# Splitting the weights into their two parts by instructions of 1024 columns instead of 512

## Chip, cores and metric

The kernel runs on one core of a Trainium2 chip. The metric is the device time of one execution in microseconds (us), lower is better; a comparison goes by the median of several runs on one chip.

## The reference

`reference()` runs two transformer blocks, batch 1, 256 tokens of width 2048, all in fp32:

```python
# first_block, two layers, a latent stream x and a context stream ctx
hx = _rmsnorm(x, norm_g[l]) * (1.0 + scale) + shift
q, k, v, g_att, u_pool, g_pool, a_conv, b_conv, g_conv = jnp.split(hx @ w_in[l], SPLITS, axis=-1)
y = _mix(...)   # attention, pooling (w_pool) and convolution, gated, joined, then @ w_out
x = x + gate * y
...
# second_block, one layer
proj = h @ w_in[l]            # q, k, v, u, gates
merged = (jax.nn.sigmoid(gate_a) * (y_attn @ w_attn_br[l])
          + jax.nn.sigmoid(gate_s) * (y_ssm @ w_ssm_br[l]))
x = x + g1[:, None] * (merged @ w_out[l])
up = causal_dwconv(h2 @ w_up[l], conv_w[l], conv_b[l])
val, gt = jnp.split(up, 2, axis=-1)
x = x + g2[:, None] * ((jax.nn.silu(gt) * val) @ w_down[l])
```

The modulation vectors (`shift`, `scale`, `gate`) come from small products of a conditioning vector with `w_mod`. What costs time are the big matrix products with `w_in`, `w_out`, `w_up` and `w_down`.

## The kernel before

Every large product is computed to nearly fp32 accuracy with the faster fp32r matmul: a weight `w` is split into a rounded part `hi` and the rest `lo = w - hi`, the tokens likewise into `xh` and `xl`, and three products are added, `xh hi + xh lo + xl hi`. All weights are streamed. A **chunk** is 4 k-tiles of 128 rows by 512 columns (1 MB); `plan()` (L500) lists 370 of them in the order in which they are used. SyncE's queue loads a chunk into a tile `wr` (three buffers); then `_split_job` (L352) makes the tiles `wh` and `wl` (two buffers each). It goes over the four k-tiles: a copy of 512 columns on ScalarE (`act`, L168) writes `wh`, a subtraction on VectorE (`sub`, which calls `tt`, L172) reads `wr` and `wh` and writes `wl`. `chunk_b` (tokens stationary) and `chunk_a` (weights stationary) then issue the chunk's matmuls (`mm`, L153) on TensorE into PSUM banks named `mm`; with 256 tokens such a chunk is 24 matmuls of 512 columns or 32 of 512 and 256.

Beside the chunks run generators: attention heads (`attn_unit`, small PSUM banks named `sd`), the pooling branch (`pool_group`), the convolution, the S5 scan, the modulation vectors (`mod_section`: products of 1024 columns on VectorE into a tile `mv`, L192), the transpositions (`tr`, L159). All of them put instructions on the same in-order queues of TensorE, VectorE, ScalarE and GpSimd; small loads go through GpSimd's queue (`dma`, L148).

The order is fixed while the program is written, by a rough clock per engine. Each helper adds an estimate (`_adv`, L128): a ScalarE instruction 0.2 us plus columns/1150, a VectorE instruction 0.2 us plus columns/960. After each step of a chunk `pump()` (L246) lets those generators go on whose due time has come, but only while the clocks of VectorE and ScalarE are at most 2 us ahead of TensorE's. `ensure()` (L262) lets them go on until a needed value exists. `_split_later` puts the split of the next chunk into the order some 5 us ahead of its use. So the estimate that a split adds to two clocks decides beside which chunk, and in which sequence, the rest is issued:

```python
            ok = t["dve"] <= t["pe"] + slack and t["act"] <= t["pe"] + slack
...
        yield max(self.ready[k] - 1.0, self.t["pe"] + self.SPLIT)
```

The output projection `out_proj` (L1981) takes the gated outputs of the branches as its tokens. It starts with the k-tiles 8 to 11, those of the pooling branch, whose four groups run one after the other; a group ends with the matmul by its block of `w_pool`, which GpSimd's queue loads into a tile `m` (L1808), and a ScalarE copy. At the start of a layer (`pre`, `inputs`) the normed tokens are made two k-tiles at a time, by a product (L172), a ScalarE copy (L168) and an L192 step of VectorE each, just ahead of the matmuls that use them; there a chunk's matmuls go k-tile by k-tile, all four column blocks of one before the next, and elsewhere column block by column block.

Of the kernel before, what the change touches and what calls it, by code (L numbers as in the profile page):

```python
# [43 lines left out]
class Core:  # L44
    """Emission helpers: engine wrappers that keep a rough clock per engine,
    the weight stream, and generators that fill the engines beside the GEMMs."""
# [24 lines left out]
    # ---- storage  # L71
# [7 lines left out]
    def N(self, n, kind):  # L79
        """A slot of 512 columns, or half of one shared with the next tile of its kind."""  # L80
        if n == 512:
            return self.S()[:, :]
        t = self.halves.pop(kind, None)
        if t is not None:
            return t[:, 256:512]
        t = self.halves[kind] = self.S()
        return t[:, 0:256]
# [39 lines left out]
    # ---- clocks  # L127
# [10 lines left out]
    def dma_at(self, kbytes, at=0.0):  # L138
        """Rough arrival of a load of so many KB issued now."""
# [3 lines left out]
    def dma(self, out, in_, eng=None):  # L143
        """A transfer beside the weight stream; returns its rough arrival."""
# [6 lines left out]
    # ---- engines  # L151
# [59 lines left out]
    def pow_half(self, out, a):  # L211
        """out = a ** -0.5 on a few columns."""
        n = _cols(a)
# [18 lines left out]
    # ---- generators  # L232
    def side(self, gen, prio, free=False):
        """free: the generator leaves ScalarE and VectorE alone."""
# [27 lines left out]
    def ensure(self, flag):  # L262
        """Run the generators, as their steps come due, until one raises the flag."""
        n = 0
# [48 lines left out]
    # ---- weight stream  # L313
# [14 lines left out]
    RAW = 3  # L328
# [23 lines left out]
    def _split_job(self, i):  # L352
# [5 lines left out]
        for k in range(self.KC):  # L358
            h = slice(k, k + 1)
# [6 lines left out]
    def fetch(self, key):  # L366
        """The two parts of the chunk of key. Loads run up to RAW chunks ahead, and
        splits one."""
        i = self.index[key]
# [13 lines left out]
    # ---- GEMM pieces over one chunk of k-tiles and 512 columns  # L383
    def chunk_b(self, key, ps, kts, lhs, first, last, evac, pre=None):
        """Tokens stationary, weights moving: one bank [128 tokens, 512] per token tile."""
# [21 lines left out]
    def chunk_a(self, key, ps, kts, xs, first, last, evac, wide, pre=None):  # L407
        """Weights stationary: four banks of 128 columns each. xs(kt) gives (H, L) of
        512 tokens when wide, else the tile [H | L] of 256 tokens."""
# [28 lines left out]
    def total(self, ps, out=None):  # L438
        """Sum of the two halves a narrow type-A bank holds; frees the bank. Without
        out the sum stays in the first half of the tile returned."""  # L440
# [8 lines left out]
    # ---- accurate functions on small tiles  # L449
    def exp_acc(self, out, x, w):  # L450
        """out = exp(x); w(): scratch tiles of x's shape, wi(): int32 scratch."""
# [20 lines left out]
    def sincos(self, s, c, x, w):  # L472
        """s = sin(x), c = cos(x) with the argument reduced to one period."""
# [14 lines left out]
class Net(Core):  # L488
# [10 lines left out]
    # ------------------------------------------------------------ plan of weights  # L499
# [58 lines left out]
    # ------------------------------------------------------------ small vectors as columns  # L558
# [74 lines left out]
    # ------------------------------------------------------------ modulation vectors  # L633
# [7 lines left out]
    def mod_section(self, key, w, bias, vec):  # L641
        """Row vector vec @ w + bias: products and the sum over k-tiles on the vector
        engine, the sum over partitions on the tensor engine. The row is left in DRAM."""
# [42 lines left out]
    def bias_rows(self, bias):  # L686
        """A row in four blocks, block j on partitions 32 j .. 32 j + 31."""
# [5 lines left out]
    def rows_out(self, rows, ps, bt):  # L693
        """Row 32 j + i of the bank, the bias added, is block j of rows[i]."""
# [6 lines left out]
    def mod_section_pe(self, keys, w, bias):  # L701
        """Rows l1[:, :, i] @ w + bias on the tensor engine, four column blocks side by
        side in the four column groups of the array."""
# [35 lines left out]
    def mod_columns(self, keys):  # L739
        """Rows in DRAM -> columns [128, 16 per key]."""  # L740
# [17 lines left out]
    def fold_scale(self, k, g):  # L758
        """scale column <- g * (1 + scale)."""
# [50 lines left out]
    # ------------------------------------------------------------ start  # L810
# [202 lines left out]
    def row_columns(self, acc, d):  # L1013
# [3 lines left out]
        row = self.S()  # L1017
# [1554 lines left out]
```

## Time and profile before

| | us |
|---|---|
| median of 3 runs | 2985.97 |
| lowest, highest run | 2984.51, 2991.15 |
| profiled execution, from its first to its last instruction | 2987.5 |
| TensorE busy in it | 2935.2 (98%) |
| VectorE busy in it | 2085.4 (70%) |
| ScalarE busy in it | 1418.9 (47%) |
| GpSimd busy in it | 460.6 (15%) |

The page lists no time of its own for the profiled execution beside the span. A row of the timeline reads: start, length, engine, line, operation, tiles out<-in, shape, number in the group, and in brackets the idle time of the engine ahead of it with what ended it. Matmuls are pipelined, so their lengths overlap; what one costs is the distance from start to start.

### The profile page before, as it was taken

The page shows a single profiled execution, that of the slowest core. Times are in us where ns is not written, and L with a number is a line of the kernel's source. Part 1 is how long each engine was busy: PE and PEld are TensorE (multiplying, and loading weights), DVE is VectorE, ACT ScalarE, POOL GpSimd, SP SyncE. Part 2 cuts the span into 40 slices and gives each one's busy share as a digit, 9 for nine tenths or more (in the row PEclk, how much of TensorE's full clock was granted, in tenths as well). Part 3 has the DMA queues.
Part 4 walks back from the last instruction along what each step waited for, and adds up shares of the span by engine and source line. Part 5 has one row for each costly group of instructions (what it writes and reads, how often), then busy time and mean ns, then how long its engine had stood idle before and what let it go on. Part 6 is the DMA issues. An engine that isn't in the chain of part 4 may idle for free.

```text
span 2987.5 us, 40758 instructions
## 1 busy us (share of the span) xinstructions
PE 2935.2 (98%) x14636; PEld 2312.9 (77%) x14636; DVE 2085.4 (70%) x3839; ACT 1418.9 (47%) x3183; POOL 460.6 (15%) x915
## 2 busy tenths in 40 slices
PE   7999999999999999999998999999999999999999
PEld 4666667777777788788776888888778888888887
DVE  4447786635776589757786888878978777777444
ACT  4333223375452443456667554444446556555343
POOL 2000000342421000334223533200000000000000
PEclk9999999999999999999998999999999999999999
DMA  9768882426677553447686877788895555556664
GB/s 378 272 225 308 304 298 74 134 99 206 220 255 254 183 196 113 144 174 238 208 292 228 288 267 270 271 289 305 294 323 194 184 194 186 187 194 226 196 198 141
DMA packets 294534, 673.20 MB, mean 225 GB/s; under 512 B 22618, under 2 KB 23334, under 8 KB 294076
## 3 DMA queue, kind: packets, MB, share of 16 engines
q1 hardware_dynamic: 266240, 604.03, 59.6%
q0 software_dynamic: 23696, 59.53, 6.0%
q10 hardware_dynamic: 4396, 7.03, 0.6%
q8 instruction: 115, 1.88, 0.3%
q14 instruction: 87, 0.71, 0.1%
HBM read 643.65 MB, written 26.85 MB: 224 GB/s over the span
## 4 chain that ended last, share of the span: by engine, by line
PE 49%; issue 1%; DVE 1%; POOL 1%; DMA 0%; ACT 0%; POOLq 0%
PE mm L153 47%; PE sd L153 2%; PE sd L159 1%; DMA m<-in_w_pool_dram 0%; DVE s L172 0%; DVE wl L172 0%; DVE s L192 0%; POOL s L1387 0%; POOL s5w L148 0%; POOL s L148 0%; POOL rstd L214 0%; POOL s L222 0%; ACT s L168 0%; POOL c L229 0%; DVE mv L192 0%
## 5 line engine op out<-in xcount | busy, mean ns | idle before, releaser
L153 PE MATMUL mm<-wh,s 128*128 128x512 f32 x4160 | 1361.5, 401 | 2.4 <-ACT s L168 2.1
L172 DVE TENSOR_TENSOR wl<-wr,wh 128x512 fp32r<-128x512 f32 x1480 | 924.3, 686 | 502.7 <-ACT wh L168 497.4
L168 ACT ACTIVATE wh<-wr 128x512 fp32r<-128x512 f32 x1480 | 810.8, 621 | 809.7 <-PE mm L153 615.8
L153 PE MATMUL mm<-s,wh 128*128 128x512 f32 x2992 | 1034.8, 400 | 9.0 <-DVE s L192 6.2
L153 PEld LDWEIGHTS mm<-wh,s 128*128 128x128 f32 x4160 | 783.1, 188 | 214.0 <-issue 21.5
L153 PE MATMUL mm<-wl,s 128*128 128x512 f32 x2080 | 822.7, 396 | 0.0
L153 PE MATMUL mm<-s,wl 128*128 128x256 f32 (+1 forms) x2528 | 765.4, 303 | 0.0
L153 PEld LDWEIGHTS mm<-s,wh 128*128 128x128 f32 x2992 | 558.8, 190 | 189.3 <-issue 54.3
L153 PEld LDWEIGHTS mm<-s,wl 128*128 128x128 f32 x2528 | 477.7, 189 | 20.1
L153 PEld LDWEIGHTS mm<-wl,s 128*128 128x128 f32 x2080 | 392.0, 188 | 87.4 <-issue 1.0
L192 DVE SCALAR_TENSOR_TENSOR mv<-mv,vec,mv 128x1024 f32<-128x1024 f32 x210 | 268.9, 1280 | 6.2 <-DMA mv<-in_w_mod_dram 3.8
L192 DVE SCALAR_TENSOR_TENSOR s<-s,CS,s 128x254 f32<-128x254 f32 (+20 forms) x424 | 230.9, 551 | 10.9
L168 ACT ACTIVATE s<-sd 128x512 f32<-128x512 f32 (+8 forms) x298 | 114.0, 389 | 222.4 <-PE sd L159 117.6
L168 ACT ACTIVATE s<-mm 128x256 f32<-128x256 f32 (+1 forms) x220 | 101.5, 464 | 215.5 <-PE mm L153 209.8
L153 PE MATMUL sd<-s,s 128*128 128x128 f32 (+6 forms) x1248 | 184.1, 399 | 8.7 <-issue 4.9
L168 ACT ACTIVATE s<-s 128x256 f32<-128x256 f32 (+5 forms) x340 | 141.5, 442 | 86.0 <-DVE s L172 39.2
L172 DVE TENSOR_TENSOR s<-s,s 128x256 f32<-128x256 f32 (+4 forms) x304 | 148.0, 516 | 39.1 <-ACT s L168 24.8
L153 PEld LDWEIGHTS sd<-s,s 128*128 128x128 f32 (+2 forms) x1248 | 112.0, 167 | 51.7 <-issue 31.7
L172 DVE TENSOR_TENSOR s<-mm,s 128x256 f32<-128x256 f32 (+1 forms) x240 | 108.5, 481 | 50.8 <-ACT s L168 25.1
L159 PE MATMUL sd<-ident,s 128*128 128x128 f32 (+1 forms) x600 | 92.9, 276 | 16.3 <-DMA s<-in_norm_g_dram 8.6
L159 PEld LDWEIGHTS sd<-ident,s 128*128 128x128 f32 (+1 forms) x600 | 73.9, 141 | 42.1 <-issue 20.6
L218 POOL TENSOR_TENSOR c<-c,mone 128x2 f32<-128x2 f32 x56 | 49.1, 877 | 343.1 <-ACT s L168 342.8
(209 smaller groups left out, 1526.6 us busy)
## 6 DMA issues: line engine op xcount, KB each, us to landing
wr<-in_w_in_dram SPq DMA_DIRECT2D x168, 1024.0 KB, 7.0
mv<-in_w_mod_dram SPq DMA_DIRECT2D x320, 512.0 KB, 5.2
wr<-in_w_up_dram SPq DMA_DIRECT2D x88, 1024.0 KB, 5.1
wr<-in_w_out_dram SPq DMA_DIRECT2D x48, 1024.0 KB, 7.6
wr<-in_w_down_dram SPq DMA_DIRECT2D x44, 1024.0 KB, 5.2
s<-in_w_mod_dram SPq DMA_DIRECT2D x128, 256.0 KB, 5.2
s<-s5w POOLq DMA_DIRECT2D x48, 256.0 KB, 6.3
mv<-in_w_in_dram SPq DMA_DIRECT2D x16, 512.0 KB, 6.7
```

The lines of the kernel that those rows point to most:

```text
L153: self.nc.tensor.matmul(out, lhsT, rhs, start=start, stop=stop)
L159: self.nc.tensor.transpose(out, in_, self.ident[0:n, 0:n])
L168: self.nc.scalar.activation(out, in_, func, scale=scale, **kw)
L172: self.nc.vector.tensor_tensor(out, a, b, op=op)
L192: self.nc.vector.scalar_tensor_tensor(out, a, s, b, op0=op0, op1=op1)
L218: self.nc.gpsimd.tensor_tensor(out, a, b, op=op)
```

## The change

The loop of `_split_job` takes two k-tiles at a time, so that each of its instructions has 1024 columns, and there are two copies and two subtractions per chunk instead of four and four:

```diff
@@ _split_job
         t["act"] = max(t["act"], self.ready[i])
-        for k in range(self.KC):
-            h = slice(k, k + 1)
+        for k in range(0, self.KC, 2):
+            h = slice(k, k + 2)
             self.act(hi[:, h, :], raw[:, h, :])
             t["dve"] = max(t["dve"], t["act"])
             self.sub(lo[:, h, :], raw[:, h, :], hi.bitcast(F32)[:, h, :])
```

By the estimates in `act` and `tt` a split now adds 2 x (0.2 + 1024/1150) = 2.18 us to ScalarE's clock, where it added 2.58, and 2 x (0.2 + 1024/960) = 2.53 to VectorE's, where it added 2.93. So the order moves too: the same other instructions stand elsewhere, on all queues. Three places follow; the number behind a name counts tiles and differs between the two programs for the same thing.

The first place is TensorE at the end of layer 1, between the last chunk of its first half and the output projection (`mm<-wh,s` is the projection's first matmul; `m` the block of `w_pool`, or an attention output to be transposed). Before:

```order
L153 MATMUL mm_13173<-s_9192,wl_13250 128x256
L153 MATMUL sd_13413<-s_11482,s_13314 128x128
...
L159 MATMUL sd_13439<-ident,m_13293 128x128
L159 MATMUL sd_13459<-ident,m_13437 128x128
L159 MATMUL sd_13296<-ident,m_13433 128x128
L153 MATMUL sd_13468<-s_13319,m_13430 128x256
L153 MATMUL mm_13477<-wh_13342,s_13403 128x512
```

Now, first the pooling matmul (some five chunks earlier, after chunk 118 where it stood after chunk 122), then the passage to the projection:

```order
L153 MATMUL mm_12452<-s_8900,wl_12598 128x256
L153 MATMUL sd_12735<-s_12582,m_12671 128x256
L153 MATMUL mm_12749<-s_8710,wh_12683 128x512
...
L153 MATMUL sd_12962<-s_11111,s_12918 128x128
L159 MATMUL sd_12741<-ident,m_12907 128x128
L153 MATMUL mm_12777<-s_8897,wh_12876 128x512
...
L153 MATMUL mm_12786<-s_8900,wl_12877 128x256
L153 MATMUL mm_13029<-wh_12935,s_13015 128x512
```

The last pooling matmul and the last transposition of attention stood directly ahead of the projection; now other matmuls stand between. On GpSimd's queue the load of the `w_pool` block stood behind the projection's loads:

```order
L148 DMA s_13320<-in_const_inv_dram 128x256
L222 MEMSET s_13322 128x16 x2
L148 DMA s_13395<-row_gate_x 128x512
L148 DMA s_13397<-x_0_7501 128x512
L148 DMA s_13399<-x_1_7502 128x512
L148 DMA s_13401<-in_final_g_dram 128x512
L148 DMA m_13430<-in_w_pool_dram 128x128
```

Now:

```order
L148 DMA s_12583<-in_const_inv_dram 128x256
L222 MEMSET s_12585 128x16 x2
L229 TENSOR_SCALAR c_12619<-c_12619 128x1
L214 TENSOR_TENSOR c_12620<-c_12619,mhalf 128x1
L218 TENSOR_TENSOR c_12620<-c_12620,c_12239 128x1
L148 DMA m_12671<-in_w_pool_dram 128x128
```

The load is issued ahead of the projection's.

The second place is VectorE in layer 1, at the splits of chunks 76 to 78, ahead of the sums of finished banks (`s<-mm,s`). Before:

```order
L192 SCALAR_TENSOR_TENSOR mv_8583<-mv_9253,vec_145,mv_8583 128x1024
L172 TENSOR_TENSOR wl_9389<-wr_9272,wh_9388 128x512 x4
L192 SCALAR_TENSOR_TENSOR mv_8583<-mv_9323,vec_145,mv_8583 128x1024
L172 TENSOR_TENSOR wl_9436<-wr_9331,wh_9435 128x512 x4
L192 SCALAR_TENSOR_TENSOR mv_8583<-mv_9336,vec_145,mv_8583 128x1024
L192 SCALAR_TENSOR_TENSOR mv_8583<-mv_9374,vec_145,mv_8583 128x1024
L172 TENSOR_TENSOR s_9451<-mm_9274,s_9451 128x256
```

Now:

```order
L192 SCALAR_TENSOR_TENSOR mv_8316<-mv_8955,vec_145,mv_8316 128x1024
L192 SCALAR_TENSOR_TENSOR mv_8316<-mv_8971,vec_145,mv_8316 128x1024
L172 TENSOR_TENSOR wl_9088<-wr_8979,wh_9087 128x1024 x2
L192 SCALAR_TENSOR_TENSOR mv_8316<-mv_9032,vec_145,mv_8316 128x1024
L172 TENSOR_TENSOR wl_9131<-wr_9034,wh_9130 128x1024 x2
L192 SCALAR_TENSOR_TENSOR mv_8316<-mv_9058,vec_145,mv_8316 128x1024
L172 TENSOR_TENSOR s_9142<-mm_8981,s_9142 128x256
```

One modulation product of 1024 columns instead of two stands between the split and the sums.

The third place is VectorE later in the same layer, at the splits of chunks 113 and 114, where an attention head's softmax (`s<-s,c,s`, then the row maxima `c<-sd` of the next head) meets the sums of finished banks. Before:

```order
L172 TENSOR_TENSOR wl_12586<-wr_12397,wh_12585 128x512 x4
L192 SCALAR_TENSOR_TENSOR s_12538<-s_12539,c_12566,s_12538 128x512
L200 TENSOR_REDUCE c_12622<-sd_12561 128x1
L200 TENSOR_REDUCE c_12622<-sd_12562 128x1
L172 TENSOR_TENSOR wl_12640<-wr_12454,wh_12639 128x512 x4
L172 TENSOR_TENSOR s_12656<-mm_12399,s_12656 128x256
```

Now:

```order
L172 TENSOR_TENSOR wl_12185<-wr_11996,wh_12184 128x1024 x2
L196 COPY m_12223<-s_12066 128x128
L192 SCALAR_TENSOR_TENSOR mv_11204<-mv_12070,vec_145,mv_11204 128x1024
L192 SCALAR_TENSOR_TENSOR s_12052<-s_11966,s_12052 128x256
L172 TENSOR_TENSOR wl_12262<-wr_12100,wh_12261 128x1024 x2
L192 SCALAR_TENSOR_TENSOR s_12212<-s_12213,c_12240,s_12212 128x512
L172 TENSOR_TENSOR s_12274<-mm_12003,s_12274 128x256
L172 TENSOR_TENSOR s_12287<-mm_12020,s_12287 128x256
L200 TENSOR_REDUCE c_12303<-sd_12292 128x1
```

The softmax step and the maxima stood ahead of the second split; now the softmax step stands behind it and the maxima behind the sums.

## Rows read from the trace of the kernel before

**Rows 1.** The page: busy time, share of the span and instructions of each engine.

```profile
PE 2935.2 (98%) x14636; PEld 2312.9 (77%) x14636; DVE 2085.4 (70%) x3839; ACT 1418.9 (47%) x3183; POOL 460.6 (15%) x915
```

**Rows 2.** Windows: each engine's busy time, then TensorE's clock, DMA share, GB/s.

```profile
1079.60:1083.00 3.40, 3.40 (x9) 2.72 (x9) 2.52 (x6) 2.48 (x6) 0.00 (x0) 0.50 0.76 272
1420.90:1427.80 6.90, 6.64 (x29) 3.79 (x30) 4.36 (x8) 1.20 (x4) 4.94 (x11) 0.51 0.47 91
1492.60:1496.00 3.40, 3.40 (x8) 2.76 (x9) 2.88 (x7) 0.98 (x3) 0.00 (x0) 0.50 0.29 57
2400.00:2450.00 50.00, 50.00 (x288) 43.80 (x287) 35.83 (x71) 30.43 (x65) 0.00 (x0) 1.00 0.58 190
```

**Rows 3.** Groups by line and form: count, busy us, mean ns, idle before, releasers.

```profile
L172 DVE TENSOR_TENSOR wl<-wr,wh 128x512 fp32r<-128x512 f32 x1480 | 924.3, 686 | 502.7 <-ACT wh L168 497.4 <-PE sd L153 3.3 <-PE mm L153 0.4
L168 ACT ACTIVATE wh<-wr 128x512 fp32r<-128x512 f32 x1480 | 810.8, 621 | 809.7 <-PE mm L153 615.8 <-issue 177.3 <-DMA wr<-in_w_out_dram 11.2
L172 DVE TENSOR_TENSOR s<-s,s 128x512 f32<-128x512 f32 x72 | 49.5, 691 | 3.5 <-ACT s L168 1.5
L168 ACT ACTIVATE s<-s 128x256 f32<-128x256 f32 x108 | 43.8, 429 | 27.7 <-DVE s L192 13.2 <-DVE s L172 7.6 <-DVE s L188 6.8
L172 DVE TENSOR_TENSOR s<-s,s 128x256 f32<-128x256 f32 x108 | 43.8, 420 | 12.3 <-DMA s<-in_const_inv_dram 11.3
L168 ACT ACTIVATE s<-s 128x512 f32<-128x512 f32 x56 | 34.8, 625 | 35.2 <-DVE s L172 31.6 <-DVE s L188 3.1
```

**Rows 4.** Timeline of ScalarE, VectorE and TensorE at one split, chunk 73.

```profile
1044.94 2.18 ACT L168 ACTIVATE wh<-wr 128x512 fp32r<-128x512 f32 x4
1045.59 2.50 DVE L172 TENSOR_TENSOR wl<-wr,wh 128x512 fp32r<-128x512 f32 x4
1046.89 0.39 PE L153 MATMUL mm<-s,wh 128*128 128x512 f32 x1
1047.12 0.28 PE L153 MATMUL mm<-s,wl 128*128 128x256 f32 x1
```

**Rows 5.** Timeline of VectorE and TensorE at the split of chunk 74.

```profile
1051.26 2.49 DVE L172 TENSOR_TENSOR wl<-wr,wh 128x512 fp32r<-128x512 f32 x4
1052.96 0.28 PE L153 MATMUL mm<-s,wl 128*128 128x256 f32 x1
```

**Rows 6.** Timeline of TensorE at the end of layer 1.

```profile
1490.64 0.44 PE L159 MATMUL sd<-ident,m 128*128 128x128 f32 x2 [2.60 <-ACT m L168]
1492.59 1.18 PE L153 MATMUL sd<-s,m 128*128 128x256 f32 x2 [1.51 <-DMA m<-in_w_pool_dram]
```

**Rows 7.** Chain that ended last, same place: start, length, what.

```profile
1483.50 8.95 DMA m<-in_w_pool_dram
```

**Rows 8.** Timeline of VectorE and TensorE at the sums behind chunk 78.

```profile
1072.84 2.60 DVE L192 SCALAR_TENSOR_TENSOR mv<-mv,vec,mv 128x1024 f32<-128x1024 f32 x2
1079.02 0.50 PE L153 MATMUL mm<-wh,s 128*128 128x512 f32 x1 [2.12 <-ACT s L168]
```

**Rows 9.** Timeline of TensorE at 1439 us: a short idle time.

```profile
1439.25 0.47 PE L153 MATMUL mm<-s,wh 128*128 128x512 f32 x1 [0.38 <-DVE s L172]
```

**Rows 10.** Timeline of VectorE and TensorE behind the splits of chunks 113 and 114.

```profile
1417.08 1.28 DVE L200 TENSOR_REDUCE c<-sd 128x1 f32<-128x512 f32 x2
1418.28 2.49 DVE L172 TENSOR_TENSOR wl<-wr,wh 128x512 fp32r<-128x512 f32 x4
1421.16 2.40 PE L153 MATMUL sd<-s,s 64*128 64x512 f32 x4 [2.19 <-DVE s L172]
```

**Rows 11.** Timeline of VectorE and TensorE where block 2 hands over to its FFN.

```profile
2233.84 2.49 DVE L172 TENSOR_TENSOR wl<-wr,wh 128x512 fp32r<-128x512 f32 x4
2237.40 1.72 PE L153 MATMUL sd<-ident,rstd 128*128 128x128 f32 x4 [2.44 <-POOL rstd L214]
```

**Rows 12.** Timeline of TensorE behind a small burst that breaks the stream of matmuls.

```profile
2106.74 0.48 PE L153 MATMUL mm<-wh,s 128*128 128x512 f32 x1
2107.06 0.39 PE L153 MATMUL mm<-wl,s 128*128 128x512 f32 x1
```

## The prediction

> **What bounds the kernel now.** I read the page first. TensorE is busy 98% of the span, VectorE 70%, ScalarE 47% [rows 1]: 2987.5 - 2935.2 = 52 us without TensorE work is all that any change on the other engines can remove, plus what a lowered clock costs. Then the windows: in the FFN TensorE is busy 50.00 of 50 us at the full clock while VectorE has work for 35.83 and ScalarE for 30.43 [rows 2]. So where most of the time passes, the split is hidden. In the groups by line VectorE's split stands idle 502.7 us, nearly all of it for `wh`, and ScalarE's 809.7 us, most of it for a buffer that TensorE gives back [rows 3]: both wait for others, and TensorE's list of waits shows none on `wl`. What a change of the split can touch is then the handful of places where TensorE stood still. There the loss is double: behind a stall the granted clock fell to 0.50, the lower of its two levels, for 3.4 to 6.9 us [rows 2], and half of such a stretch is lost too.
>
> **The instructions themselves.** Going from 256 to 512 columns, a ScalarE copy grows from 429 to 625 ns and a VectorE operation from 420 to 691 [rows 3]. With the same slope the next 512 columns cost 392 and 542 ns: a copy of 1024 about 621 + 392 = 1013 ns, a subtraction 686 + 542 = 1228. From start to start four copies take (2.18 - 0.62)/3 = 0.52 us each and four subtractions (2.50 - 0.69)/3 = 0.60 [rows 4]; at 1024 that is 0.91 and 1.15. A chunk needs 2.08 -> 1.83 us of ScalarE and 2.42 -> 2.29 of VectorE, over 370 chunks 93 and 48 us less. I cost this at nothing: the rest of the stream's matmuls hides it, the idle time above.
>
> [...]
>
> **What comes later.** The parts are handed over in pieces. Counted from the start of the first copy, the four pieces of `wl` are ready at 1.34, 1.94, 2.55 and 3.15 us now [rows 4]. In two pieces the first is ready at 1.04 + 1.23 = 2.27, the second at 3.42. That is harmless where a split is done long ahead. It is tight at chunk 73, where the inputs of layer 1 are being made: the split starts at 1044.94 and the first `lo` is wanted at 1047.12, that is at 2.18 [rows 4], so 2.27 is 0.09 late; the second piece is wanted two k-tiles of 1.4 us later and is in time. The next tightest I read is chunk 74, where VectorE starts at 1051.26, behind other work, with `wh` already there: the pieces would end 1.23 and 1.15 + 1.23 later, at 1052.49 and 1053.64; they are wanted at 1052.96 and, two k-tiles of 0.35 on, at 1053.66 [rows 5], just in time. I take **+0.1**, with 0 (should splits start earlier) and 13 x 0.09 = 1.2 (all 13 chunks that are split beside the making of inputs as tight as this one) as ends.
>
> **What moves.** The order is the larger part, since the planner's clocks of two engines change by 0.40 us per chunk.
>
> 1. *End of layer 1.* TensorE waited 2.60 us for an attention output and then 1.51 for the block of `w_pool` [rows 6], a load issued at 1483.50 that landed 8.95 us later [rows 7], and the clock was 0.50 for the next 3.4 us [rows 2]. In the new order the pooling matmul stands five chunks earlier, its load ahead of the projection's loads, and a dozen matmuls follow the last transposition. Both waits go: -4.1, and half of 3.4 us: **-5.8**. What is late next is the evacuation of that last transposition, which 12 matmuls (some 2 us) now cover. At worst half of the 2.60 comes back and the clock falls as before: -2.8.
> 2. *Chunk 78.* TensorE waited 2.12 us for a chain that ends in ScalarE and starts behind two modulation products of 1.30 us each [rows 8]. One stays: -1.3. The 0.8 that remain I expect not to lower the clock, since TensorE went on at full speed behind the 0.38 at 1439 us [rows 9]; half of 3.4 us [rows 2] is 1.7. **-3.0**, between 0 and -3.8.
> 3. *Chunk 114.* TensorE waited 2.19 us for a sum on VectorE that stood behind a split, and this behind two maxima of together 1.2 us [rows 10]. The maxima now stand behind the sums: **-1.2**. I don't credit the 6.9 us at half clock [rows 2], because a burst of small matmuls follows anyway. Ends: -2.2 - 3.45 = -5.6, and +0.5 if the softmax step, now ahead of the sums, waits for GpSimd.
> 4. *Hand-overs between layers.* At the two boundaries, at 1600 and 2235 us, a split stands ahead of the statistics of the next norm [rows 11]. It shortens by 0.13 to 0.2 each: **-0.3** (-0.8 to +0.2).
> 5. *Breaks.* In the new order the stream of matmuls is broken 347 times instead of 336. One break costs 0.09 us: the second matmul behind it starts 0.32 later instead of 0.23 [rows 12]. **+0.3**, between 0 and 11 x 0.09 = +1.0.
> 6. *Bursts in block 2.* S5 and attention pieces stand closer together around chunks 166 and 175, in long runs without a large matmul between. **+0.5** (0 to +17, see the third rival).
>
> Sum with the +0.1 above: -9.4. The profiled execution took 2987.5 us, 1.5 above the median and within the runs' spread; 2987.5 - 9.4 = 2978.1, and by the median's scale 2985.97 - 9.4 = **2976.6**.
>
> **Rivals.** A change under 0.2%, 6 us, is about what this kernel's measurement can't tell from none.
>
> *Hidden anyway.* The waits at 1, 2 and 3 are replaced by as many new ones elsewhere, since the planner knows only its estimates and not the waits of the trace. Then only the shorter instructions are left, and they lie under TensorE's work: about 2984 to 2987, no change. For it speaks that the moved instructions are the same in number; against it that the new order unpicks the three places, as its rows show. 0.20.
>
> *Late pieces.* By this mechanism every chunk that is split just ahead of its use pays: the 13 chunks where the inputs of a layer are made while its first matmuls run (71 to 76, 128, 141 to 146). Each pays up to the 2.27 - 1.34 = 0.93 us by which the first piece is later: 12.1 in place of my 0.1, which gives 2988.6, no change. Against it: only the tightest of them, chunk 73, comes out late at all above, and by 0.09. 0.12. [...] VectorE at 70% [rows 1] is not saturated in this trace, and its list of waits of TensorE shows no bubble from the split.
>
> *Bursts.* In block 2 a run of transpositions and S5 matmuls depends, within the run, on a ScalarE copy of its own transpositions. If that copy stands behind a split pair, now 1.83 us in two long instructions, TensorE waits as at the end of layer 1: 2.6 us and 1.7 of clock. At two places with two dependences each that is 4 x 4.3 = 17 us: 2976.6 + 17 = 2994, slower. It decides where the copy isn't through within the small matmuls between. Against it: the ScalarE order has the copies at chunk 166 ahead of the next split. 0.16.
>
> *It doesn't do what it says.* If 1024 columns cost twice 512 (1372 ns), the engines save nothing, the pieces are later still by 0.1 to 0.3 us each (+0.5 in all at most), and the terms of order stay: 2977, faster. The slopes in rows 3 speak against it. 0.07.
>
> **Numbers.** My forecast has 0.45. Faster than 2980.0: 0.40 of it, 0.06 of the last rival and 0.04 of the first, 0.50. Within: 0.05 of the forecast, 0.15 of the first rival, 0.11 of the second and 0.01 of the last, 0.32. Slower than 2991.9: 0.16 and the rest of the first two, 0.18. Downward the range takes items 1 to 4 at their gaining ends, -5.8 - 3.8 - 5.6 - 0.8 = -16, to 2970; upward it takes in the first two rivals and the third with three of its four waits (2976.6 + 13 = 2990), to 2991. The forecast by itself holds 2970 to 2983.
>
> **What would show it.** Right: 740 copies of about 1.01 us and 740 subtractions of about 1.23; no wait for `m<-in_w_pool_dram` and no half clock at the end of layer 1; at most 1 us at chunk 78, with the full clock behind it; no wait of TensorE for `wl` beyond 1 us in all. Wrong: several new waits of over 2 us in TensorE's list, each with a stretch at half clock behind it, above all in block 2 between 1700 and 1950 us; or waits on `wl` at the 13 chunks.

## The result and the profile after

The change makes the kernel slower. Four runs of the changed kernel have a median of 3007.23 us (3006.05 to 3009.68), four of the kernel before 2987.59; the ratio is 1.0061, 95% interval 1.0048 to 1.0074. A second measurement later gave 1.0046 (1.0030 to 1.0061). So the loss is 14 to 18 us where I had forecast a gain of 9.

The page of the changed kernel, its span and its line on the engines, answers to [rows 1]:

```profile
span 3005.4 us, 39332 instructions
...
PE 2941.9 (98%) x14636; PEld 2316.2 (77%) x14636; DVE 2037.7 (68%) x3099; ACT 1353.7 (45%) x2443; POOL 476.6 (16%) x915
```

VectorE and ScalarE do have less to do, 48 and 65 us less. TensorE pays: the part of the span in which it is not busy rose from 52.3 to 3005.4 - 2941.9 = 63.5 us, +11.2, and its busy time for the same 14636 instructions by 6.7.

The groups by line, against [rows 3]:

```profile
L172 DVE TENSOR_TENSOR wl<-wr,wh 128x1024 fp32r<-128x1024 f32 x740 | 873.7, 1222 | 599.7 <-ACT wh L168 591.6 <-PE mm L153 6.2 <-DMA mv<-in_w_mod_dram 1.4
L168 ACT ACTIVATE wh<-wr 128x1024 fp32r<-128x1024 f32 x740 | 742.4, 1052 | 873.1 <-PE mm L153 676.1 <-issue 167.4 <-DMA wr<-in_w_out_dram 11.7
```

1222 and 1052 ns: the subtraction is what the slope said (1228), the copy 39 ns longer (1013), so ScalarE saves 65 us and not 93.

TensorE's list of waits for the changed kernel (total us, times, longest):

```profile
PE mm L153 <- ACT s L168: 8.9, 5, 3.8
...
PE mm L153 <- DVE s L172: 7.5, 4, 4.7
...
PE sd L153 <- DMA m<-in_w_pool_dram: 2.6, 2, 2.5
...
PE mm L153 <- DVE wl L172: 1.5, 3, 0.8
```

Before, the first two were 4.6 and 0.6 us, the load 1.5, and there was no entry for `wl`. The waits at my first three places fell, from 8.4 us together (2.12, 2.19, 2.60 and 1.51) to 3.9 (1.17, 0.52, 0.53 and 1.69). Some 16 us of new waits at other places outweigh that. The two longest are these, in the timelines of VectorE, ScalarE and TensorE. At chunk 126, where the output projection's tokens are made:

```profile
1511.80 1.12 DVE L172 TENSOR_TENSOR s<-s,s 128x256 fp32r<-128x256 f32 x3
1512.84 0.75 DVE L172 TENSOR_TENSOR s<-s,s5p 128x256 f32<-128x256 f32 x2
...
1517.31 0.42 DVE L172 TENSOR_TENSOR s<-s 128x256 f32<-128x256 f32 x1
1517.65 0.42 DVE L192 SCALAR_TENSOR_TENSOR s<-s,s 128x256 f32<-128x256 f32 x1
1518.10 0.42 ACT L168 ACTIVATE s<-s 128x256 fp32r<-128x256 f32 x1 [0.62 <-DVE s L192]
1518.57 0.51 PE L153 MATMUL mm<-wh,s 128*128 128x512 f32 x1 [3.20 <-ACT s L168]
```

Three of the chunk's four token tiles are finished by 1512.9. Then twelve instructions for the S5 weights, eight products with `s5p` and four sums, stand in VectorE's queue ahead of the gating product of the fourth (1517.65), for which TensorE waits. And at chunk 216, where the tokens of block 2's second branch are made:

```profile
2099.47 2.38 DVE L172 TENSOR_TENSOR wl<-wr,wh 128x1024 fp32r<-128x1024 f32 x2
2101.75 1.97 DVE L192 SCALAR_TENSOR_TENSOR s<-s,s 128x256 f32<-128x256 f32 x3
2103.63 2.60 DVE L192 SCALAR_TENSOR_TENSOR mv<-mv,vec,mv 128x1024 f32<-128x1024 f32 x2
2106.15 0.67 DVE L192 SCALAR_TENSOR_TENSOR s<-s,s 128x256 f32<-128x256 f32 x1
2106.74 1.27 DVE L192 SCALAR_TENSOR_TENSOR mv<-mv,vec,mv 128x1024 f32<-128x1024 f32 x1
2107.93 1.42 DVE L172 TENSOR_TENSOR s<-s,s 128x256 fp32r<-128x256 f32 x4
2108.40 1.22 PE L153 MATMUL mm<-wh,s 128*128 128x512 f32 x2 [4.68 <-DVE s L172]
```

Three modulation products of 1.3 us each stand between the gating products and the subtractions that TensorE needs. The kernel before has none there and TensorE waited 0.20 us:

```profile
2097.27 0.73 PE L153 MATMUL mm<-wh,s 128*128 128x512 f32 x2 [0.20 <-DVE s L172]
```

The windows of the changed kernel show the price of the clock behind such waits, against [rows 2]: no half clock at chunk 78 and behind a new wait of 2.45 us at chunk 112 (the second row), 3.4 us of it at the end of layer 1 and at chunk 126, 6.8 at chunk 216. The last row is a stretch of the FFN:

```profile
1085.00:1088.40 3.40, 3.21 (x14) 2.50 (x15) 2.37 (x5) 2.25 (x6) 0.00 (x0) 1.00 0.92 343
1421.40:1424.80 3.40, 3.40 (x21) 3.05 (x22) 1.08 (x2) 2.53 (x4) 0.00 (x0) 1.00 1.07 366
1495.40:1498.80 3.40, 3.40 (x10) 2.62 (x9) 3.37 (x6) 2.50 (x7) 0.00 (x0) 0.50 0.58 227
1519.30:1522.70 3.40, 3.40 (x10) 2.63 (x9) 3.17 (x4) 1.11 (x2) 3.40 (x7) 0.50 0.72 181
2106.40:2113.20 6.80, 4.80 (x11) 3.80 (x12) 5.35 (x9) 2.31 (x3) 0.00 (x0) 0.50 0.86 297
2420.00:2470.00 50.00, 50.00 (x284) 43.50 (x284) 36.22 (x57) 27.57 (x43) 0.00 (x0) 1.00 0.56 190
```

In the FFN, against the last of [rows 2], TensorE is as busy as before and at full clock, without a wait, and yet gets through 284 matmuls in 50 us instead of 288. By the start times of the matmuls, three pairs (512 and 256 columns each) repeat every 1060 ns, as here over 27 pairs:

```profile
2319.96 0.40 PE L153 MATMUL mm<-s,wh 128*128 128x512 f32 x1
2329.50 0.39 PE L153 MATMUL mm<-s,wh 128*128 128x512 f32 x1
```

The kernel before has 1060 ns too at the start of the FFN (15 pairs in 5.30 us), and 1047 behind a small burst at 2312.02 (6 pairs in 2.09 us):

```profile
2305.92 0.40 PE L153 MATMUL mm<-s,wh 128*128 128x512 f32 x1
2311.22 0.40 PE L153 MATMUL mm<-s,wh 128*128 128x512 f32 x1
2312.02 0.64 PE L153 MATMUL sd<-mv,ones 128*32 128x256 f32 x8
2313.05 0.40 PE L153 MATMUL mm<-s,wh 128*128 128x512 f32 x1
2315.14 0.40 PE L153 MATMUL mm<-s,wh 128*128 128x512 f32 x1
```

Behind that place the up projection has some 400 such triples: 400 x 13 ns = 5.2 us.

So of the 17.9 us between the two spans 11.2 are TensorE's idle time and 5.2 the FFN's rhythm. The clock adds nothing in sum: the stretches at half clock come to 54.5 us in either profile, only at other places. The remaining 1.5 us I did not trace.

### The profile page after: what moved, and what is told of

Its sections match the earlier page's. It is cut to its first block, busy times and chain, and to the rows that moved or that the text cites. A ratio compares the mean times of both kernels' runs of the same rounds, so it can differ in the third digit from the quotient of the medians.

```text
span 3005.4 us, 39332 instructions
## 1 busy us (share of the span) xinstructions
PE 2941.9 (98%) x14636; PEld 2316.2 (77%) x14636; DVE 2037.7 (68%) x3099; ACT 1353.7 (45%) x2443; POOL 476.6 (16%) x915
## 4 chain that ended last, share of the span: by engine, by line
PE 72%; DVE 2%; issue 1%; POOL 1%; ACT 1%; DMA 0%; POOLq 0%; ACTq 0%; DVEq 0%
PE mm L153 67%; PE sd L153 4%; PE sd L159 2%; DVE s L172 1%; DVE wl L172 1%; ACT s L168 1%; DVE s L192 0%; POOL c L218 0%; ACT wh L168 0%; POOL c L214 0%; DVE mv L192 0%; DMA m<-in_w_pool_dram 0%; DMA s5w<-s 0%; POOL c L229 0%; POOL s L222 0%
## 5 line engine op out<-in xcount | busy, mean ns | idle before, releaser
L172 DVE TENSOR_TENSOR wl<-wr,wh 128x1024 fp32r<-128x1024 f32 x740 | 873.7, 1222 | 599.7 <-ACT wh L168 591.6
L168 ACT ACTIVATE wh<-wr 128x1024 fp32r<-128x1024 f32 x740 | 742.4, 1052 | 873.1 <-PE mm L153 676.1
L153 PEld LDWEIGHTS mm<-s,wh 128*128 128x128 f32 x2992 | 557.9, 189 | 190.0 <-issue 52.7
L159 PE MATMUL sd<-ident,s 128*128 128x128 f32 (+1 forms) x600 | 94.1, 276 | 17.9 <-DMA s<-in_norm_g_dram 8.8
L148 POOL DMA_DIRECT2D s<-row_gate_x x16 | 9.0, 566 | 540.9 <-PE mm L153 493.8
```

The lines of the kernel that those rows point to most:

```text
L148: eng.dma_start(out, in_)
L153: self.nc.tensor.matmul(out, lhsT, rhs, start=start, stop=stop)
L159: self.nc.tensor.transpose(out, in_, self.ident[0:n, 0:n])
L168: self.nc.scalar.activation(out, in_, func, scale=scale, **kw)
L172: self.nc.vector.tensor_tensor(out, a, b, op=op)
```

## The experiments

Theory A: the planner's new order makes the loss. Theory B: the instructions make it, since they hand over later. Here is a table of the measurements; intervals are 95%. The two kernels with 44 bursts in the FFN (below) ran once each, for their profile, and are not in it.

| run | instructions | order | ratio to before |
|---|---|---|---|
| the change | wide | new | 1.0061 (1.0048 to 1.0074) |
| the change again | wide | new | 1.0046 (1.0030 to 1.0061) |
| wide, old order | wide | old | 1.0016 (1.0006 to 1.0027) |
| narrow, new order | narrow | new | 1.0049 (1.0035 to 1.0063) |
| wide copies only | copies wide | old | 1.0017 (1.0007 to 1.0028) |
| wide subtractions only | subtractions wide | old | 1.0016 (1.0006 to 1.0026) |
| narrow where tight | wide in 325 chunks | old | 1.0001 (0.9991 to 1.0012) |
| hold at two places | wide | new, but there | 1.0037 (1.0023 to 1.0051) |
| burst in the FFN | wide | new | 1.0051 (1.0036 to 1.0066) |
| split charged more | narrow | another | 1.0144 (1.0127 to 1.0161) |
| split charged less | narrow | another | 1.0055 (1.0036 to 1.0074) |
| early pool weights | narrow | old, one load moved | 0.9998 (0.9988 to 1.0007) |
| sums ahead of a split | narrow | old, load and 4 moved | 0.9994 (0.9984 to 1.0004) |
| before, three bursts | narrow | old | 1.0008 (0.9998 to 1.0019) |

**Order or instructions.** Two kernels cross the two. One has the wide instructions and charges the planner for narrow ones; its edit of the changed kernel:

```diff
         for k in range(0, self.KC, 2):
             h = slice(k, k + 2)
-            self.act(hi[:, h, :], raw[:, h, :])
-            t["dve"] = max(t["dve"], t["act"])
-            self.sub(lo[:, h, :], raw[:, h, :], hi.bitcast(F32)[:, h, :])
+            self.nc.scalar.activation(hi[:, h, :], raw[:, h, :], AF.Copy, scale=1.0)
+            self.nc.vector.tensor_tensor(lo[:, h, :], raw[:, h, :], hi.bitcast(F32)[:, h, :], op=ALU.subtract)
+            for _ in range(2):
+                self._adv("act", 0.2 + 512 / 1150.0)
+                t["dve"] = max(t["dve"], t["act"])
+                self._adv("dve", 0.2 + 512 / 960.0)
```

> The instructions of the change (two copies and two subtractions of 1024 columns), but the planner's clocks are advanced as if there were four of 512, so that every queue keeps the order of the kernel before. Theory A (the loss comes from the moved order, not from the instructions): within 4 us of the kernel before, no wait of TensorE over 1 us that the kernel before doesn't have, at chunk 73 a wait on wl of at most 0.6 us, and the FFN's three pairs of matmuls at 1047 ns as before. Rival B (pieces handed over later make TensorE wait): about 18 us above the kernel before, with the long waits of the changed kernel.

The other has the narrow instructions and charges for wide ones; its edit is the mirror image.

> The reverse: four copies and four subtractions of 512 columns as before, but the planner's clocks are advanced as for two of 1024, so that every queue has the order of the changed kernel. Theory A: as slow as the changed kernel, 14 to 20 us above the kernel before, with waits of about 3 us at chunk 126 and 4 to 5 us at chunk 216 and the FFN's three pairs at 1060 ns. Rival B: within 4 us of the kernel before.

Measured: 1.0016 and 1.0049, that is 5 and 15 us. The new order without the wide instructions has the waits of the changed kernel, in TensorE's timeline at chunks 126 and 216:

```profile
1517.58 0.50 PE L153 MATMUL mm<-wh,s 128*128 128x512 f32 x1 [3.04 <-ACT s L168]
2106.37 1.22 PE L153 MATMUL mm<-wh,s 128*128 128x512 f32 x2 [4.67 <-DVE s L172]
```

A measure that does not contain the FFN's rhythm says the same: TensorE's time without work in the profile (span less busy time). In the old order it is 52.3 to 54.9 us in five kernels with narrow instructions (before, early pool weights, sums ahead of a split, three bursts, 44 bursts) and 58.3 to 58.8 in four with wide ones (wide old order, copies only, subtractions only, 44 bursts). In the new order it is 64.4 with narrow instructions and 63.5 and 64.9 with wide ones, where they cost nothing further. So theory A holds: by the ratios the new order alone is four fifths of the loss of the first measurement and all of that of the second, by the idle time all of it. Rival B, 18 us from the instructions, falls. But the wide instructions are not free in the old order, and 5 us is more than the 4 that theory A allowed. (In the FFN that run's profile had 1060 ns, not 1047 as expected; more on this below.) The timelines of VectorE and TensorE of that run show two of the places (the split's lines are 360 and 361 in it):

```profile
1029.72 2.36 DVE L361 TENSOR_TENSOR wl<-wr,wh 128x1024 fp32r<-128x1024 f32 x2 [0.46 <-ACT wh L360]
1032.00 0.15 DVE L204 TENSOR_REDUCE c<-ss_o 128x1 f32<-128x4 f32 x1
1033.86 0.50 PE L153 MATMUL mm<-s,wh 128*128 128x512 f32 x1 [1.03 <-DVE s L192]
1047.80 0.39 PE L153 MATMUL mm<-s,wl 128*128 128x256 f32 x1 [0.66 <-DVE wl L361]
```

At chunk 73 (1047.80) TensorE waits for the piece itself. At chunk 71 it waits for something that stands behind the split in VectorE's queue: the split there began at 1029.37 in the kernel before and begins 0.35 later, since the first copy takes longer (1052 ns on average, 621 for a narrow one), and the layer's inputs behind it are late. The trace of the kernel before shows no wait at either place, but it is not a good measure here: TensorE ran at half clock just ahead of them and came late. In the four other profiles of narrow instructions in this order it did not, and they have 0.73 us at chunk 71 and 0.43 to 0.46 at chunk 73. A window of the kernel before, and TensorE's timeline with early pool weights:

```profile
1028.40:1031.80 3.40, 3.40 (x13) 2.92 (x11) 3.31 (x7) 2.50 (x6) 0.00 (x0) 0.50 0.00 0
1030.53 0.51 PE L153 MATMUL mm<-s,wh 128*128 128x512 f32 x1 [0.73 <-DVE s L192]
```

So the wide instructions add 0.2 to 0.3 us at each of the two. Other waits that are there with narrow ones grow in the same way: 2.40 instead of 2.1 us at chunk 78, 3.02 instead of 2.2 at chunk 114, 0.67 instead of 0.4 at 1439. All these come to some 2 us; the rest of the 5 was not traced.

**Which instruction.** In the next two only one of the pair is wide, with the order held.

```diff
-            h = slice(k, k + 1)
-            self.act(hi[:, h, :], raw[:, h, :])
+            h, g = slice(k, k + 1), slice(k, k + 2)
+            if k % 2 == 0:
+                self.nc.scalar.activation(hi[:, g, :], raw[:, g, :], AF.Copy, scale=1.0)
+            self._adv("act", 0.2 + 512 / 1150.0)
```

> The kernel before, with its order, where only ScalarE's copies have 1024 columns (two per chunk); VectorE still subtracts in four pieces. Theory E (with the order held, the rest of the loss is VectorE's first subtraction, which waits for a copy twice as long): the first subtraction starts about 0.4 us later, so the waits of TensorE around the making of inputs grow as in the first experiment (1.0 us at chunk 71, 0.6 at chunk 73), and the time rises by 2 to 5 us. Rival F (it is the long subtraction that hands over late): no more than 1 us.

```diff
-            h = slice(k, k + 1)
+            h, g = slice(k, k + 1), slice(k - 1, k + 1)
...
-            self.sub(lo[:, h, :], raw[:, h, :], hi.bitcast(F32)[:, h, :])
+            if k % 2 == 1:
+                self.nc.vector.tensor_tensor(lo[:, g, :], raw[:, g, :], hi.bitcast(F32)[:, g, :], op=ALU.subtract)
+            self._adv("dve", 0.2 + 512 / 960.0)
```

> The kernel before, with its order, where only VectorE's subtractions have 1024 columns; ScalarE copies in four pieces. Each subtraction waits for two short copies, 1.14 us instead of 1.01, so by theory E it starts later still: 2 to 5 us slower, with the waits of the first experiment. By rival F too, 3 to 6 us; the two differ on the run with wide copies alone.

Both cost as much as the pair, 1.0017 and 1.0016, with waits of 1.16 and 1.11 us at chunk 71. What they have in common is that the first subtraction must wait for more copying, so theory E holds as far as the two go; rival F, by which the wide copies alone cost nothing, falls.

**Where.** Wide instructions, old order, but narrow ones around the layers' starts and ends:

```diff
+NARROW = set(range(69, 82)) | set(range(109, 116)) | set(range(121, 130)) | set(range(138, 148)) | set(range(212, 218))
...
+        w = 1 if i in NARROW else 2
+        for k in range(0, self.KC, w):
+            h = slice(k, k + w)
```

> Wide instructions with the order of the kernel before, as in the first experiment, but the 46 chunks around the layers' starts and ends (70 to 82, 110 to 116, 122 to 130, 139 to 148, 213 to 218) keep their four narrow ones; 324 chunks are wide. If the loss of the wide instructions lies in those stretches: within 2 us of the kernel before, and TensorE's waits there as before (chunk 71 0.7, chunk 73 none on wl, 2.1 at chunk 78). If it is spread over all chunks: still 4 to 6 us slower.

The trace has 180 subtractions of 512 columns and 650 of 1024, so it is 45 narrow chunks and 325 wide ones. 1.0001: the loss of the wide instructions lies in these 45 chunks, and in the other 325 they cost and bring nothing beyond the interval of some 3 us either way. So, with the order held, narrow instructions in these chunks are worth the 5 us (1.0001 against 1.0016).

**The two long waits.**

```diff
             yield ready[i]
+            while self.nf in (125, 215):
+                yield
...
             for k in range(1, 5):
+                while self.nf in (125, 215):
+                    yield
```

> The changed kernel, but the generators of the modulation products and of the S5 output weights do no step while the tokens of chunk 126 and of chunk 216 are being made, so that VectorE has nothing else in front of these tokens. Theory A: the waits of 3.20 and 4.68 us and the half clock behind them (3.4 and 6.8 us) go, 3.2 + 1.7 + 4.7 + 3.4 = 13 us below the changed kernel, less what the order behind these places brings by chance (3 us either way). Rival (these waits have another cause, such as late pieces or loads): less than 4 us below.

The first wait goes and the second shrinks to 1.03 us, so what the two generators put ahead on VectorE was their cause. The span falls from 3005.4 to 2999.2 (both with 1060 ns in the FFN): 6.2 us, half of the 13; by the medians it is 4 to 8, so the times alone don't rule out the rival. Of the 6.2 TensorE's busy time gives 5.1, as much as the half clock behind the two waits had cost ((3.4 + 6.8) / 2). Its time without work fell by only 1.1, to 62.4: most of the 7.9 us of waits came back, as the timeline of TensorE shows one chunk ahead of chunk 216 and there:

```profile
2095.57 0.73 PE L153 MATMUL mm<-wh,s 128*128 128x512 f32 x2 [1.61 <-DVE s L172]
2100.69 0.73 PE L153 MATMUL mm<-wh,s 128*128 128x512 f32 x2 [1.03 <-DVE s L172]
```

**Is there a direction in the charge?** Narrow instructions, with 0.1 us more (the edit shown) or 0.05 less on each in the planner's clocks:

```diff
             self.act(hi[:, h, :], raw[:, h, :])
+            t["act"] = t["act"] + 0.1
             t["dve"] = max(t["dve"], t["act"])
             self.sub(lo[:, h, :], raw[:, h, :], hi.bitcast(F32)[:, h, :])
+            t["dve"] = t["dve"] + 0.1
```

> The kernel before, but the planner charges each instruction of a split 0.1 us more, 2.98 us of ScalarE and 3.33 of VectorE per chunk instead of 2.58 and 2.93. Theory A1 (the less a split is charged, the more other work the planner puts on VectorE ahead of what TensorE needs): not slower than the kernel before, by 0 to 8 us faster, with fewer waits of TensorE for VectorE and ScalarE. Theory A2 (any other order is a new draw): anywhere between 8 us faster and 20 us slower, with long waits at other places.

> The kernel before, but the planner charges each instruction of a split 0.05 us less, 2.38 us of ScalarE and 2.73 of VectorE per chunk, half of what the change took off. Theory A1: between the kernel before and the changed order, 5 to 12 us slower than before. Theory A2: anywhere between 8 us faster and 20 us slower.

A1 falls. The dearer charge is much slower, 1.0144, 43 us and so beyond the 20 of A2 too; TensorE's timeline has the longest wait of the study, for a modulation row that isn't ready:

```profile
2171.02 1.08 PE L153 MATMUL sd<-mv,ones 128*32 128x256 f32 x8 [12.61 <-DVE mv L192]
2177.44 0.31 PE L159 MATMUL sd<-ident,m 32*128 32x32 f32 x1 [5.34 <-DMA m<-row_shift_x]
```

The cheaper one has 1.0055, 16 us, as A2 allows. Three new orders were tried, on both sides of the old charge, and all three lose 14 to 43 us: the old one is better than any of them. Whether that is chance, or the rest of the program had been fitted to the old order, no run shows.

**The rhythm of the FFN.** The changed kernel has no small burst in the FFN; the kernel before has the one at 2312.02, behind which 1060 ns turned into 1047.

```diff
+                if key == ("gt", 1, 0) and n == 0 and j == 0:
+                    d = self.sd()
+                    one = self.ones2[:, 0:1].to_broadcast([128, 32])
+                    for i in range(4):
+                        self.nc.tensor.matmul(d[32 * i:32 * i + 32, 0:256], one, x.bitcast(F32)[:, 0:256], start=True, stop=True)
```

> The changed kernel with one burst of four small matmuls, whose result is not used, behind the first pair of matmuls of the FFN's 13th chunk, where the kernel before has such a burst and the changed kernel has none. Theory C (TensorE's matmuls run in one of two locked rhythms, three pairs in 1047 or in 1060 ns, and only an interruption changes the rhythm): from there on 1047 ns, 16 pairs x 4.3 ns x 75 chunks = 5.2 us less, 0.7 us for the burst: 4 to 5 us below the changed kernel. Rival (the rhythm comes from something else, such as the wide instructions' traffic): 1060 ns stays and the time rises by 0.7 us.

The burst did change the rhythm, but the other way: 1047 ns ahead of it (in the same instructions that ran at 1060 in the first profile) and 1060 behind it. So the rhythm is not the program's alone. The next two draw it 44 times, with the same burst in every second chunk of the up projection:

> The kernel before (four instructions of 512 columns) with a burst of four small matmuls, whose result is not used, in every second chunk of the FFN's up projection: 44 interruptions, each a draw of TensorE's rhythm (three pairs in 1047 or in 1060 ns). Theory D (the rhythm behind an interruption is chance and has nothing to do with the split): both rhythms occur, each in 10 to 34 of the 44 stretches. Rival (narrow instructions give the fast rhythm, wide ones the slow): at least 40 of 44 fast. The time is of no interest; the bursts cost some 30 us.

> The same bursts in the kernel with two instructions of 1024 columns and the order of the kernel before. Theory D: as many fast stretches as with narrow instructions, within 10 of 44. Rival: at least 40 of 44 slow (1060 ns).

Narrow: 16 fast stretches of 44. Wide: 16 of 44 whole stretches too. So the width of the split's instructions does not set it. Nor is it chance from burst to burst: with 32 pairs between bursts both go slow, slow, fast, slow, slow, fast, from the 10th stretch to the end. One more run tried to steer it, with bursts in three successive chunks:

> The kernel before with three bursts of four small matmuls (results not used) in three successive chunks of the FFN, 16 pairs apart. In the runs with bursts, a stretch of 16 pairs behind a fast one was again followed by a fast one. If three bursts lead to the fast rhythm from any start: 1047 ns from there on in every execution, 2 us for the bursts, and executions that lie closer together than those of the kernel before (13 us from lowest to highest). Otherwise 1060 ns in the profile and the same scatter.

In the profile it stayed at 1060 ns behind all three, and the runs scatter by 13 us as before: three bursts do not steer it. Last, the changed kernel again:

> The changed kernel once more, for a second profile of the same program and more runs. If the FFN's rhythm belongs to the execution: one in three of such profiles has 1047 ns, and the runs scatter over 5 us or more; if it belongs to the program: 1060 ns again and runs within 4 us. The waits of 3.2 us at chunk 126 and 4.7 us at chunk 216 stand there again in either case. 15 to 19 us above the kernel before.

This time the FFN ran at 1047 ns from its start, without any burst, and the same program took 2996.3 us in its span instead of 3005.4. Of these 9.1 us the rhythm gives 6.1 (469 triples x 13 ns):

```profile
2420.00:2470.00 50.00, 50.00 (x288) 43.80 (x288) 34.63 (x53) 27.07 (x42) 0.00 (x0) 1.00 0.58 190
```

The waits at chunks 126 and 216 are there again (3.21 and 4.67 us). The runs lie in two groups, 2998.0 to 3000.5 and 3006.5 to 3007.8; the profile at 1047 ns is of the first and the one at 1060 of the second. The four runs of the first measurement all lay where the second group does, 3006 or more. If the rhythm makes the groups, which two profiles suggest and don't show, that was bad luck, and the loss is nearer to 14 us than to 18. Of the 15 profiles with no or few bursts, six had 1047 ns in most of the FFN and nine 1060, with narrow and wide instructions in both. The runs of the kernel before beside these reach from 2982.4 to 2994.9, and all ratios above carry this scatter.

**A version that beats both?** With the old order held, single waits of the kernel before were taken away: first the late load of `w_pool`,

```diff
+        wp = self.S()[:, 0:128]
+        self.nc.gpsimd.dma_start(wp, self.io["w_pool"][l, g])
...
-        wp = self.mid()
-        self.dma(wp[:, :], self.io["w_pool"][l, g])
+        self._adv("pool", 1.04)
+        self.dma_at(64)
```

> The kernel before, with its order, but each group's w_pool block is loaded at the group's start into another buffer instead of at its end behind the output projection's loads. If TensorE's wait for that load at the end of layer 1 (1.5 to 2.4 us) is worth its length: 1.5 to 2.5 us faster than before, and the wait of 2.60 us for the attention output ahead of it stays. If the load only hid another wait: no change.

then also the split of chunk 114 put behind two sums:

```diff
         self.nc.vector.tensor_tensor(out, a, b, op=op)
+        if self.defer and self.count and _is_psum(a):
+            self.count -= 1
+            if not self.count:
+                self.flush()
...
+            if i == 113:
+                self.defer += ((lambda h=h: self.nc.vector.tensor_tensor(
+                    lo[:, h, :], raw[:, h, :], hi.bitcast(F32)[:, h, :], op=ALU.subtract)),)
+                self.count = 2
...
```

> The kernel before with the early load of w_pool, and on VectorE the four subtractions of chunk 114 stand behind the two sums that free the banks for which TensorE waited 2.19 us, instead of ahead of them; every other instruction keeps its place. The wait goes but for 0.2 us: 2 us less, and up to 3.4 us more where the clock does not fall behind it: 2 to 5 us faster than the kernel before. If the wait comes back at the next place on the way: no change.

0.9998 and 0.9994, neither to be told from 1; the intervals leave room for a gain of 4 or 5 us. The profiles show none in TensorE's time without work, 52.7 and 54.3 us against 52.3. Both waits are gone and others have taken their place, in TensorE's timeline of the last run:

```profile
1423.37 0.50 PE L153 MATMUL mm<-s,wh 128*128 128x512 f32 x1 [1.85 <-DVE s L180]
...
1485.35 0.44 PE L159 MATMUL sd<-ident,m 128*128 128x128 f32 x2 [2.60 <-ACT m L168]
1490.67 0.50 PE L153 MATMUL mm<-wh,s 128*128 128x512 f32 x1 [2.34 <-ACT s L168]
```

The 2.19 us at 1421 became 1.85 at 1423, for a sum on VectorE (line 180 in this kernel), and the 1.51 for the load became 2.34 for the tokens behind it (0.77 in the run with the early load alone). No version that is faster than the kernel before was found.

## Why the prediction was wrong

- *The step that failed* is the choice of places: "What a change of the split can touch is then the handful of places where TensorE stood still." I followed the new order only where the trace of before had a wait, that is where a new order can only help, and where TensorE's own queue changed. But it puts other work ahead of what TensorE needs at any place. The two longest new waits, 3.20 and 4.68 us, stand on VectorE's queue at chunks 126 and 216, where tokens are made just ahead of their use and little or nothing was lost before (0.20 us at chunk 216). New waits came to some 16 us, the half clock behind these two to 5.1. That the waits "are replaced by as many new ones elsewhere" was a rival, but I gave it no net loss; all three new orders that were tried lose.
- *Items 1 to 3 of the moved order*, -10: by the two profiles these places gave nearly that, 4.5 us of waits and 5.1 of clock (3.4 us at half clock instead of 13.6). That the sum agrees is luck, for not every item does. The end of layer 1 gave 1.9 of 5.8: 2.2 us of waits (0.53 and 1.69) are left of 4.1, and the half clock stayed. Chunk 78 gave 2.7 of 3.0: 1.17 us is left, with the full clock behind it. Chunk 114 gave 5.1 for 1.2: 0.52 us is left, and the half clock behind it, which I had not credited, is gone. And the load of `w_pool` was late after all, for another group: 2.45 us at chunk 112, where its matmul stands a chunk earlier than before.
- *Items 4 to 6*: too small to be told apart in the measured time. The bursts in block 2, my slower rival, cause no wait between 1700 and 1950 us; the kernel is slower as that rival said, but from another place.
- *The instructions themselves*: right in what counts, the time saved on VectorE and ScalarE is hidden. The copy was 1052 ns and not 1013.
- *What comes later*, +0.1: too small with the order held, about +5, where I had the end of the range at 1.2; in the new order it adds nothing that the profiles show. I took the time at which `lo` is wanted, 2.18 us behind the start of the split, from a profile in which TensorE came late to chunk 73 behind a half clock. In the four other profiles of narrow instructions in this order it is wanted at 1.65 to 1.67, so a piece that is ready at 2.27 is late by 0.6 us and not 0.09, as with the wide instructions it was (0.66). And I did not count what stands behind the split on VectorE, the layer's inputs at chunk 71 (1.0 us instead of 0.7) and the sums and tokens at the places further on.
- *The rhythm* of the FFN, +5 us in the first measurement, was in no view that I read as a risk, though the kernel before shows both rhythms in its own trace.

## What to carry to other kernels

Where a planner with estimated clocks sets the order, an edit of a cost can move the whole program, as each of three edits did here (14 to 43 us lost): hold the order fixed to learn what the edit itself does, and compare the new order at every place where something is made right ahead of its use, not only where the old trace waited. With the order held, larger instructions on VectorE (busy 70% of the span before) and ScalarE (47%) brought nothing here (1.0001 where 325 chunks had them), and cost where the first piece was waited for (0.66 us at chunk 73) or where other urgent work stood behind them (1.03 at chunk 71). A wait that was taken away alone was worth far less than its length here, as another had been hidden behind it: in three runs most of it came back or turned up elsewhere (with two waits of together 7.9 us held off, TensorE's time without work fell by 1.1). And one profile is one execution: a stretch at half clock that other executions don't have can hide a wait, as the 3.4 us of it ahead of chunk 71 did with the 0.73 us that the four others show there.

## What the hardware showed that I had not expected

In the FFN of these profiles the stream of alternating matmuls of 512 and 256 columns ran, at full clock and without a wait, in one of two rhythms: three pairs in 1047 or in 1060 ns. In all traces it stayed in one for as long as nothing else stood between, up to the 1408 pairs of the whole up projection (1060 ns in the changed kernel, 1047 when it ran again), and changed only at an interruption. Which one follows is open: with 32 pairs between bursts the two repeat as slow, slow, fast, but four bursts 16 pairs apart (the three and the kernel's own) were each followed by the slow one, and the same program starts its FFN with either. In the FFN here that is 5 to 6 us, part of the 13 us by which executions of the same program differ. What inside TensorE repeats with three pairs was not found.

The clock followed the waits less strictly than I had assumed: behind 2.12 us of waiting at chunk 78 it fell to the lower level for 3.4 us before, and behind 2.45 us at chunk 112 it stayed at the upper level in the changed kernel; behind 3.2 and 4.68 us it fell for 3.4 and 6.8 us.
